# An attention layer on one core: output products held one block behind their transposes, group splits spread, weight subtraction in halves

## The chip, the core and the metric

The kernel runs on one core of a Trainium2 chip. Five engines work in parallel, each through its own queue in order: TensorE (PE, matmuls and transposes; its weight loads are shown as PEld), VectorE (DVE), ScalarE (ACT), GpSimd (POOL) and SyncE (SP, which issues the loads and stores here). SBUF is the working memory; TensorE writes to PSUM, in banks of 128 x 512 float32. The metric is the time of one execution on the device in microseconds; lower is better.

## The reference

One layer of native sparse attention on x of 512 x 1024, float32. With u = RMSNorm(x), a projection gives 16 query heads of 64, three key/value pairs (compressed, selected, window) for 4 groups, gates, and a SiLU path z. With 512 tokens and blocks of 64, all eight blocks are selected, so "selected" is plain causal attention, as is the window of 512.

```
q, kv, g, z = split(u @ w_in)
kc, vc      = compress_kv(k_c, ...), compress_kv(v_c, ...)      # 31 blocks
for branch in (cmp, slc, win):
    p = masked_softmax(q k^T / 8 + bias(distance))
    o[branch] = p v
y   = sum over branches of sigmoid(g) * o * silu(z)
out = x + RMSNorm_post(y @ w_out)
```

## The kernel before

Float32 products are made of two halves: every operand is split into a rounded high part h and the rest l = raw - h, and a product is h*h + l*h + h*l, three matmuls (L144 to L146 for the projections, L809 to L811 for the output). A weight tile of 128 x 1024 is loaded by SP (L103), cast to h (L113 on ScalarE, L115 on VectorE) and subtracted to l (L116). After 126 us the casts are ScalarE's and the subtractions GpSimd's; before, every second tile is VectorE's alone. L425 is one of the three matmuls with which the hidden layer of compress_kv uses such a tile (l times the block).

The attention goes through 28 units: 4 groups of (win 3, win 2, win 1, both 0, slc 1, slc 2, slc 3), where the number is the block of 128 queries; the last group takes its slc units as 3, 2, 1. `qk(u)` makes the scores of four heads (L589), the masked minimum (L601, VectorE) and the exponential (L602, ScalarE), then the factor f (L646) and the widened f times gate (L648, VectorE, two inputs in SBUF). `pv(u)` takes the unit before. For each block j of 128 keys it transposes four heads' probabilities into a PSUM bank (L681), casts them to `pth` (L684, ScalarE), subtracts to `ptl` (L685, VectorE), and multiplies with v (L689 with pth, L690 with ptl) into an accumulator `acc`, which has one bank (`ob`). Product j - 1 is issued behind the transposes of block j; the product of the last block follows in the same unit, behind the two transposes of f (L695). Then ScalarE copies halves of the accumulator out (L700, L701), VectorE adds (L702, L703), and GpSimd multiplies with zs and adds into y (L706, or L708 and L709). `cmp_pv` does the same for the compressed branch behind unit "both" (L752 transposes, L755 cast, L760 to L762 products); `cmp_prep` readies its softmax (L745 is a product of 128 x 16 on VectorE, L746 the one on GpSimd). `split_y` casts and subtracts a quarter of a group's y for the output projection (L777 ScalarE, L778 VectorE); groups 0 to 2 do four quarters in a row behind their last unit.

`weave` alternates the steps of qk(i) and pv(i - 1). Each step yields a cost, and between steps the main loop pulls as many filler steps (projections of later groups, then the output projection `wout`) as a clock of such costs asks for. A tile framework then orders each engine's queue, near the order of the program. A zs tile (three buffers) is free again when `zdone` has its branch.

Of the kernel before, what the change touches and what calls it, by code (L numbers as in the profile page):

```python
# [19 lines left out]
S = 512  # L20
# [4 lines left out]
R = 4  # L25
# [26 lines left out]
def nsa_layer(ctx: ExitStack, tc: tile.TileContext, x, pre_gain, post_gain, table, w_in, w_out,  # L52
# [53 lines left out]
    def split_raw(raw, kn, eh, el, home=None):  # L106
# [9 lines left out]
        el.tensor_tensor(l[:, 0:kn], raw[:, 0:kn], h[:, 0:kn].bitcast(F32), op=ALU.subtract)  # L116
# [547 lines left out]

    def pv(u):
        g, kind, qt = u
        if u == units[g * 7]:
            yt[g] = at.tile([128, 2, S], F32, name="y", tag="y", bufs=1)
        y = yt[g]
        qsl = slice(qt * 128, (qt + 1) * 128)  # L670
        for st in state.pop(u):
            br = st["br"]
            zf = zs[g, br][:, :, qsl]
            acc = ob()
            prev = None
            for j in range(qt + 2):
                if j <= qt:
                    c = st["o"] + j * 128
                    tp = tb()
                    for hh in range(R):  # L680
                        T.transpose(tp[:, hh * 128:(hh + 1) * 128], st["p"][hh][:, c:c + 128], ident)  # L681
                    ph = at.tile([128, S], F32R, name="pth", tag="pth", bufs=2)
                    pl = at.tile([128, S], F32R, name="ptl", tag="ptl", bufs=2)
                    A.copy(ph, tp)  # L684
                    V.tensor_tensor(pl, tp, ph.bitcast(F32), op=ALU.subtract)  # L685
                    yield 690, 440
                if prev is not None:
                    v = vt[:, prev[0], br - 1, g, :]
                    T.matmul(acc, v, prev[1], start=j == 1, stop=False)  # L689
                    T.matmul(acc, v, prev[2], start=False, stop=j == qt + 1)  # L690
                    yield 0, 450
# [5 lines left out]
                prev = (j if br == B_WIN else qt - j, ph, pl)  # L697
            tmp = at.tile([128, 2, 128], F32, name="otmp", tag="otmp", bufs=3)
            av = acc.rearrange("p (a e q) -> p a e q", a=2, e=2)
            A.copy(tmp[0:64], av[64:128, :, 0])  # L700
            A.copy(tmp[64:128], av[0:64, :, 1])  # L701
            V.tensor_tensor(tmp[0:64], av[0:64, :, 0], tmp[0:64], op=ALU.add)  # L702
            V.tensor_tensor(tmp[64:128], av[64:128, :, 1], tmp[64:128], op=ALU.add)  # L703
            eng = V if u == units[-1] else P
            if br == B_WIN:
                eng.tensor_tensor(y[:, :, qsl], tmp, zf, op=ALU.mult)  # L706
            else:
                eng.tensor_tensor(tmp, tmp, zf, op=ALU.mult)  # L708
                eng.tensor_tensor(y[:, :, qsl], y[:, :, qsl], tmp, op=ALU.add)  # L709
            yield 1250, 220  # L710
        if kind == "both":
            zdone.add((g, B_WIN))
            yield from cmp_pv(g)
            zdone.add((g, B_CMP))
            if g == 3:
                split_y(g, 0)
# [31 lines left out]
    def cmp_pv(g):  # L748
        lc, y, vb = lcs[g], yt[g], vbs[g]
# [173 lines left out]
    for i in range(len(units) + 1):  # L923
# [53 lines left out]
```

## Time and profile before

| | us |
|---|---|
| median of 3 runs (lowest to highest) | 479.68 (478.58 to 480.18) |
| profiled execution, its own time | 476.7 |
| span from first to last instruction of that execution | 474.9 |
| TensorE busy | 453.8 |
| VectorE, ScalarE, GpSimd busy | 328.6, 272.3, 178.3 |

In the span, the time before about 11 us is start-up, to about 126 us are the projections and the compression, to about 453 us the units with their filler, and the rest is the end of the output projection. Granted TensorE clock: 0.995 over the span. A row of a timeline has the start, the duration, the engine, the line and the operation with the tiles written and read; idle time ahead of it and what ended it stand in brackets. A matmul is drawn longer than the distance to the next one, since they are pipelined.

### The profile page before, as it was taken

How to read it: one execution, taken by the hardware profiler on the slowest of the kernel's cores; microseconds unless marked ns; L12 is line 12 of the kernel's file. 1: busy time of each engine (PE TensorE's matmuls, PEld its weight loads, DVE VectorE, ACT ScalarE, POOL GpSimd, SP SyncE). 2: the span in 40 equal slices, each digit the busy share in tenths (PEclk: the TensorE clock that was granted, in tenths of full speed). 3: DMA queues.
4: the chain of work that ended last, by engine and by line, in shares of the span. 5: the costliest groups of instructions: out<-in, count | busy, mean ns of one | idle time of the engine just before them, and what ended most of it. 6: DMA issues, size and time to landing. Idle time of an engine off the chain costs nothing.

```text
span 474.9 us, 6859 instructions
## 1 busy us (share of the span) xinstructions
PE 453.8 (96%) x2330; PEld 373.6 (79%) x2330; DVE 328.6 (69%) x788; ACT 272.3 (57%) x643; POOL 178.3 (38%) x139
## 2 busy tenths in 40 slices
PE   5999999999999999999999999999999999997993
PEld 4888788878888878888877887887888887876782
DVE  6789752844667887866857866766886668576576
ACT  5613232535757678766657865755866565546531
POOL 3325543234042635151453324335333244156142
PEclk9999999999999999999999999999999999999997
DMA  8498455351120322220330502032151120124013
GB/s 296 137 88 269 144 168 170 97 176 46 44 90 19 94 88 75 104 60 30 109 92 0 174 5 90 5 108 88 46 177 46 44 85 21 72 80 144 1 44 133
DMA packets 45501, 44.63 MB, mean 94 GB/s; under 512 B 7751, under 2 KB 38471, under 8 KB 45466
## 3 DMA queue, kind: packets, MB, share of 16 engines
q1 hardware_dynamic: 44424, 44.00, 31.2%
q8 instruction: 18, 0.29, 0.2%
q10 hardware_dynamic: 1042, 0.20, 0.2%
q14 instruction: 17, 0.14, 0.1%
HBM read 41.99 MB, written 2.20 MB: 93 GB/s over the span
## 4 chain that ended last, share of the span: by engine, by line
PE 80%; DVE 9%; ACT 5%; issue 3%; POOL 1%; DVEq 0%; POOLq 0%; ACTq 0%
PE ps_pj L144 10%; PE ps_pj L146 10%; PE ps_pj L145 10%; PE ps_s L589 8%; PE ps_t L681 6%; PE ps_o L690 4%; PE ps_o L689 4%; PE ps_s L245 2%; PE ps_s L246 2%; PE ps_s L247 2%; PE ps_pj L809 2%; PE ps_pj L810 2%; PE ps_pj L811 2%; PE ps_pj L245 1%; PE ps_pj L246 1%
## 5 line engine op out<-in xcount | busy, mean ns | idle before, releaser
L116 POOL TENSOR_TENSOR wl<-wr,wh 128x1024 fp32r<-128x1024 f32 x47 | 113.6, 2417 | 147.8 <-ACT wh L113 135.1
L144 PE MATMUL ps_pj<-uh,wh 128*128 128x512 f32 x240 | 98.5, 410 | 0.0
L146 PE MATMUL ps_pj<-ul,wh 128*128 128x512 f32 x240 | 94.3, 393 | 0.0
L145 PE MATMUL ps_pj<-uh,wl 128*128 128x512 f32 x240 | 94.1, 392 | 0.0
L602 ACT ACTIVATE p<-p,nm 128x512 f32<-128x512 f32 (+3 forms) x128 | 71.7, 561 | 26.6 <-DVE nm L601 25.9
L113 ACT CAST wh<-wr 128x1024 fp32r<-128x1024 f32 x47 | 49.2, 1047 | 44.0 <-DMA wr<-in_nsa_w_in_dram 19.0
L685 DVE TENSOR_TENSOR ptl<-ps_t,pth 128x512 fp32r<-128x512 f32 x80 | 55.1, 689 | 26.0 <-ACT pth L684 25.2
L589 PE MATMUL ps_s<-kd,q 128*128 128x512 f32 (+5 forms) x256 | 62.5, 332 | 0.0
L146 PEld LDWEIGHTS ps_pj<-ul,wh 128*128 128x128 f32 x240 | 45.1, 188 | 10.2
L684 ACT CAST pth<-ps_t 128x512 fp32r<-128x512 f32 x80 | 46.0, 575 | 11.5 <-PE ps_t L681 11.1
L589 PEld LDWEIGHTS ps_s<-kd,q 128*128 128x128 f32 x256 | 44.6, 189 | 7.9
L145 PEld LDWEIGHTS ps_pj<-uh,wl 128*128 128x128 f32 x240 | 45.3, 189 | 5.6
L144 PEld LDWEIGHTS ps_pj<-uh,wh 128*128 128x128 f32 x240 | 45.2, 188 | 5.1
L681 PE MATMUL ps_t<-ident,p 128*128 128x128 f32 x320 | 48.2, 272 | 0.0
L681 PEld LDWEIGHTS ps_t<-ident,p 128*128 128x128 f32 x320 | 39.6, 140 | 9.3
L601 DVE CUSTOM_DVE_ANT_0 p<-ps_s,bias 128x128 f32<-128x128 f32 (+3 forms) x80 | 34.6, 446 | 12.0 <-PE ps_s L589 11.3
L689 PE MATMUL ps_o<-pth,vt 128*128 128x512 f32 x80 | 35.5, 444 | 1.5 <-ACT pth L684 1.2
L601 DVE CUSTOM_DVE_ANT_1 p<-ps_s,bias 128x256 f32<-128x256 f32 (+2 forms) x48 | 26.1, 552 | 14.7 <-PE ps_s L589 14.2
L690 PE MATMUL ps_o<-ptl,vt 128*128 128x512 f32 x80 | 32.8, 410 | 3.3 <-DVE ptl L685 3.3
L706 POOL TENSOR_TENSOR y<-otmp,zs 128x256 f32<-128x256 f32 x16 | 11.8, 738 | 57.2 <-DVE otmp L703 57.2
L708 POOL TENSOR_TENSOR otmp<-otmp,zs 128x256 f32<-128x256 f32 x15 | 11.0, 736 | 45.9 <-DVE otmp L703 45.9
L702 DVE TENSOR_TENSOR otmp<-ps_o,otmp 64x256 f32<-64x256 f32 x32 | 13.3, 416 | 18.6 <-ACT otmp L701 17.6
(268 smaller groups left out, 892.8 us busy)
## 6 DMA issues: line engine op xcount, KB each, us to landing
wr<-in_nsa_w_in_dram SPq DMA_DIRECT2D x36, 512.0 KB
wr<-in_nsa_w_in_dram SPq DMA_DIRECT2D x16, 256.0 KB
bias<-toepd SPq DMA_DIRECT2D x16, 256.0 KB
wr<-in_nsa_w_out_dram SPq DMA_DIRECT2D x8, 512.0 KB
xt<-in_x_dram SPq DMA_DIRECT2D x4, 512.0 KB
wr<-in_nsa_cmp_k_w_dram SPq DMA_DIRECT2D x4, 512.0 KB
wr<-in_nsa_cmp_v_w_dram SPq DMA_DIRECT2D x4, 512.0 KB
xr<-in_x_dram SPq DMA_DIRECT2D x8, 256.0 KB
```

The costliest lines, as they stand in the source:

```text
L113: A.copy(h[:, 0:kn], raw[:, 0:kn])
L116: el.tensor_tensor(l[:, 0:kn], raw[:, 0:kn], h[:, 0:kn].bitcast(F32), op=ALU.subtract)
L144: T.matmul(p, a, rh, start=k == 0, stop=False)
L145: T.matmul(p, b, rh, start=False, stop=False)
L146: T.matmul(p, a, rl, start=False, stop=k == KT - 1)
L589: T.matmul(po, qs[h][:, qt * 128:(qt + 1) * 128], kds[h // R][:, i, c0:c0 + n], start=i == 0, stop=i == 1)
L601: V.tensor_tensor_reduce(pd, src, bi, 1.0, BIG, ALU.add, ALU.min, st["nm"][:, hh:hh + 1])
L602: A.activation(po, po, AF.Exp, bias=st["nm"][:, hh:hh + 1], scale=-1.0, accum_out=st["rs"][:, hh:hh + 1])
L681: T.transpose(tp[:, hh * 128:(hh + 1) * 128], st["p"][hh][:, c:c + 128], ident)
L685: V.tensor_tensor(pl, tp, ph.bitcast(F32), op=ALU.subtract)
L689: T.matmul(acc, v, prev[1], start=j == 1, stop=False)
L690: T.matmul(acc, v, prev[2], start=False, stop=j == qt + 1)
```

## The change

Four things change. (1) pv no longer issues a product itself: it puts it in `hold`, and the next block's `flush(0)` issues it behind that block's transposes, also when the next block is another branch's or the next unit's; what follows the last product (copies, additions, zdone, splits) goes with it. The compressed product is held in the same way. (2) The four splits of a group are put in `owed` with counts 1 to 4 and are traced one per block in the units that follow, each queued behind that block's cast on ScalarE. The splits of the last group stay with the product. (3) The weight subtraction is two instructions on two of the four 256-column pieces each, on GpSimd as on VectorE. (4) The costs yielded are the same in sum and lie elsewhere. Banks and buffers are as they were.

```
-        el.tensor_tensor(l[:, 0:kn], raw[:, 0:kn], h[:, 0:kn].bitcast(F32), op=ALU.subtract)
+        for k in range(0, kn, 2):
+            ks = slice(k, k + 2)
+            el.tensor_tensor(l[:, ks], raw[:, ks], h[:, ks].bitcast(F32), op=ALU.subtract)
...
+    hold, owed = [], []
+    def flush(n):
+        while len(hold) > n:
+            yield from hold.pop(0)()
     def pv(u):
...
-            for j in range(qt + 2):
-                if j <= qt:
+            for j in range(qt + 1):
...
-                    A.copy(ph, tp)
+                cast = A.copy(ph, tp)
+                V.tensor_tensor(pl, tp, ph.bitcast(F32), op=ALU.subtract)
+                yield 690, 440
+                for o in list(owed):
+                    o[0] -= 1
+                    if o[0] <= 0:
+                        owed.remove(o)
+                        with tc.issue_after(cast.ins):
+                            o[1]()
+                        yield 420, 0
+                yield from flush(0)
-                if prev is not None:
-                    v = vt[:, prev[0], br - 1, g, :]
-                    T.matmul(acc, v, prev[1], start=j == 1, stop=False)
-                    T.matmul(acc, v, prev[2], start=False, stop=j == qt + 1)
-                    yield 0, 450
...
+                hold.append(lambda st=st, j=j, ph=ph, pl=pl, zf=zf: product(u, st, j, ph, pl, zf))
         if kind == "both":
+            yield from cmp_t(u)
+    def product(u, st, j, ph, pl, zf):
...
+        T.matmul(acc, v, ph, start=j == 0, stop=False)
+        T.matmul(acc, v, pl, start=False, stop=j == qt)
+        yield 0, 450
+        if j < qt:
+            return
...
         if kind == "slc":
             if g == 3:
                 split_y(g, qt)
-            elif u == units[g * 7 + 6]:
-                for t in range(NT):
-                    split_y(g, t)
-                    yield 420, 0
             if u == units[g * 7 + 6]:
+                if g < 3:
+                    owed.extend([t + 1, lambda t=t: split_y(g, t)] for t in range(NT))
                 zdone.add((g, B_SLC))
...
+        if i == len(units):
+            gens[1] = seq(gens[1], flush(0))
```

In the new kernel the products are L714 and L715 (for L689 and L690), the transposes of f L698 (L695), the scores L591 (L589), the subtraction L118 (L116), the split's cast L802 (L777), the projections L146 to L148 (L144 to L146), the output projection L834 to L836 (L809 to L811). The transposes keep L681 and the cast L684.

TensorE at the end of unit win 3 of group 1, before: the first row has the last block's transposes, `pth` in the row before L589 is that block's cast.

```order
L681 MATMUL ps_t<-ident,p 128x128 x4
L689 MATMUL ps_o<-pth,vt 128x512
L690 MATMUL ps_o<-ptl,vt 128x512
L695 MATMUL ps_s<-ident,f_2101 128x128 x2
L689 MATMUL ps_o<-pth,vt 128x512
L589 MATMUL ps_s<-kd,q 128x288 x2
L144 MATMUL ps_pj<-uh_83,wh 128x512
L145 MATMUL ps_pj<-uh_83,wl 128x512
L690 MATMUL ps_o<-ptl,vt 128x512
L146 MATMUL ps_pj<-ul_87,wh 128x512
L681 MATMUL ps_t<-ident,p 128x128 x4
```

The same place now, from the last block's transposes to those of the next unit's first block.

```order
L681 MATMUL ps_t<-ident,p 128x128 x4
L146 MATMUL ps_pj<-uh_82,wh 128x512
L147 MATMUL ps_pj<-uh_82,wl 128x512
L148 MATMUL ps_pj<-ul_86,wh 128x512
L714 MATMUL ps_o<-pth,vt 128x512
L715 MATMUL ps_o<-ptl,vt 128x512
L698 MATMUL ps_s<-ident,f_2121 128x128 x2
L591 MATMUL ps_s<-kd,q 128x288 x2
L681 MATMUL ps_t<-ident,p 128x128 x4
```

Before, the last block's first product stands four rows behind its transposes. Now the two products shown are still the block's before it; the last block's own come 15 rows below the last row shown, behind the next unit's first transposes.

TensorE at the end of unit slc 3 of group 3, where the unit that is woven with it has fewer steps; before:

```order
L689 MATMUL ps_o<-pth,vt 128x512
L690 MATMUL ps_o<-ptl,vt 128x512
L681 MATMUL ps_t<-ident,p 128x128 x4
L689 MATMUL ps_o<-pth,vt 128x512
L690 MATMUL ps_o<-ptl,vt 128x512
L695 MATMUL ps_s<-ident,f_4489 128x128 x2
L809 MATMUL ps_pj<-wh,yhl 128x512
L689 MATMUL ps_o<-pth,vt 128x512
L810 MATMUL ps_pj<-wh,yhl 128x512
```

and now:

```order
L714 MATMUL ps_o<-pth,vt 128x512
L715 MATMUL ps_o<-ptl,vt 128x512
L681 MATMUL ps_t<-ident,p 128x128 x4
L714 MATMUL ps_o<-pth,vt 128x512
L715 MATMUL ps_o<-ptl,vt 128x512
L681 MATMUL ps_t<-ident,p 128x128 x4
L714 MATMUL ps_o<-pth,vt 128x512
L698 MATMUL ps_s<-ident,f_4522 128x128 x2
L591 MATMUL ps_s<-kd,q 128x256
L715 MATMUL ps_o<-ptl,vt 128x512
```

Blocks follow each other here without filler in both; a product now has one product pair and one group of transposes between it and its own transposes.

ScalarE behind the last unit of group 1, before: `yhl` is a split's output, `otmp` the copies out of the accumulator, `wh` a weight cast. The first three splits stand further up; this is the fourth.

```order
L684 CAST pth<-ps_t 128x512
L113 CAST wh<-wr 128x1024
L700 COPY otmp<-ps_o 64x256
L701 COPY otmp<-ps_o 64x256
L567 ACTIVATE zs<-ps_pj 128x512
L777 CAST yhl<-y 128x2x128
L113 CAST wh<-wr 128x1024
L602 ACTIVATE p,rs<-p,nm 128x384
L684 CAST pth<-ps_t 128x512
```

and now, from the copies out of the same unit's accumulator:

```order
L722 COPY otmp<-ps_o 64x256
L723 COPY otmp<-ps_o 64x256
L684 CAST pth<-ps_t 128x512
L604 ACTIVATE p,rs<-p,nm 128x384
L802 CAST yhl<-y 128x2x128
L684 CAST pth<-ps_t 128x512
L802 CAST yhl<-y 128x2x128
L684 CAST pth<-ps_t 128x512
L802 CAST yhl<-y 128x2x128
L604 ACTIVATE p,rs<-p,nm 128x256
L684 CAST pth<-ps_t 128x512
L802 CAST yhl<-y 128x2x128
```

All four splits now stand behind the copies, one to a block and each behind that block's cast; the fourth, which reads the quarter of y that the unit's product completes, stands seven rows further on than the first.

More of the change, by code (lines that the diff above doesn't have):

```diff
@@ L663, in qk @@
             load_bias(g + 1)
+    hold, owed = [], []
+    def flush(n):
+        while len(hold) > n:
+            yield from hold.pop(0)()
     def pv(u):
         g, kind, qt = u
[L667 to L670, printed above, removed]
         for st in state.pop(u):
[L672 to L675, printed above, removed]
-            for j in range(qt + 2):
-                if j <= qt:
[L678 to L686, printed above, removed]
-                if prev is not None:
-                    v = vt[:, prev[0], br - 1, g, :]
-                    T.matmul(acc, v, prev[1], start=j == 1, stop=False)
-                    T.matmul(acc, v, prev[2], start=False, stop=j == qt + 1)
-                    yield 0, 450
+            zf = zs[g, st["br"]][:, :, qt * 128:(qt + 1) * 128]
+            for j in range(qt + 1):
+                c = st["o"] + j * 128
+                tp = tb()
+                for hh in range(R):
+                    T.transpose(tp[:, hh * 128:(hh + 1) * 128], st["p"][hh][:, c:c + 128], ident)
+                ph = at.tile([128, S], F32R, name="pth", tag="pth", bufs=2)
+                pl = at.tile([128, S], F32R, name="ptl", tag="ptl", bufs=2)
+                cast = A.copy(ph, tp)
[9 more added lines that the diff above has]
+                yield from flush(0)
                 if j == qt:
@@ L696, in pv @@
                     V.tensor_tensor(zf, zf, fb[:, 0:256].rearrange("p (a q) -> p a q", a=2), op=ALU.mult)
[L697 to L710, printed above, removed]
-        if kind == "both":
+                    yield 420, 220
+                hold.append(lambda st=st, j=j, ph=ph, pl=pl, zf=zf: product(u, st, j, ph, pl, zf))
@@ new lines, in pv @@
+        if kind == "both":
+            yield from cmp_t(u)
+    def product(u, st, j, ph, pl, zf):
+        g, kind, qt = u
+        br = st["br"]
+        if j == 0:
+            st["acc"] = ob()
+        if j == qt and u == units[g * 7]:
+            yt[g] = at.tile([128, 2, S], F32, name="y", tag="y", bufs=1)
+        acc, y = st["acc"], yt.get(g)
+        v = vt[:, j if br == B_WIN else qt - j, br - 1, g, :]
+        T.matmul(acc, v, ph, start=j == 0, stop=False)
[3 more added lines that the diff above has]
+            return
+        qsl = slice(qt * 128, (qt + 1) * 128)
+        tmp = at.tile([128, 2, 128], F32, name="otmp", tag="otmp", bufs=3)
+        av = acc.rearrange("p (a e q) -> p a e q", a=2, e=2)
+        A.copy(tmp[0:64], av[64:128, :, 0])
+        A.copy(tmp[64:128], av[0:64, :, 1])
+        V.tensor_tensor(tmp[0:64], av[0:64, :, 0], tmp[0:64], op=ALU.add)
+        V.tensor_tensor(tmp[64:128], av[64:128, :, 1], tmp[64:128], op=ALU.add)
+        eng = V if u == units[-1] else P
+        if br == B_WIN:
+            eng.tensor_tensor(y[:, :, qsl], tmp, zf, op=ALU.mult)
+        else:
+            eng.tensor_tensor(tmp, tmp, zf, op=ALU.mult)
+            eng.tensor_tensor(y[:, :, qsl], y[:, :, qsl], tmp, op=ALU.add)
+        yield 840, 0
+        if kind == "both" and br == B_SLC:
@@ L712, in pv @@
             zdone.add((g, B_WIN))
[L713 to L716, printed above, removed]
         if kind == "slc":
@@ L746, in cmp_prep, with cmp_t @@
         P.tensor_tensor(l3, l3, view(rs, 0, [[1, NT * R], [0, CP]]), op=ALU.mult)
[L748 to L749 removed]
+    def cmp_t(u):
+        g = u[0]
+        lc = lcs[g]
         tp = tb()
@@ L757, in cmp_pv, with cmp_product @@
         yield 680, 440
+        yield from flush(0)
+        hold.append(lambda: cmp_product(g, ph, pl))
+    def cmp_product(g, ph, pl):
+        y, vb = yt[g], vbs[g]
         for pr in range(2):
@@ L766, in cmp_pv @@
             yield 1800, 690
+        zdone.add((g, B_CMP))
+        if g == 3:
+            split_y(g, 0)
     def split_y(g, qt):
```

## The prediction, as made before the run

> **What bounds the kernel now.** I read the page's busy shares first, then the table of five stretches (columns: length, then busy time and count of each engine), then TensorE's waits between 126 and 453 us, where the attention runs.
>
> ```profile
> PE 453.8 (96%) x2330; PEld 373.6 (79%) x2330; DVE 328.6 (69%) x788; ACT 272.3 (57%) x643; POOL 178.3 (38%) x139
> 0.00:11.00 11.00, 5.71 (x18) 4.11 (x19) 6.29 (x17) 6.22 (x11) 4.70 (x13) 1.00 0.85 309
> 11.00:126.00 115.00, 113.01 (x621) 96.03 (x620) 75.22 (x124) 47.70 (x97) 41.04 (x24) 1.00 0.54 139
> 126.00:400.00 274.00, 271.81 (x1395) 223.19 (x1394) 197.99 (x561) 183.78 (x458) 101.11 (x77) 1.00 0.23 71
> 400.00:453.00 53.00, 48.80 (x240) 38.60 (x239) 33.80 (x69) 28.68 (x64) 22.62 (x15) 1.00 0.20 70
> 453.00:474.90 21.90, 14.49 (x64) 11.64 (x62) 15.30 (x21) 5.95 (x17) 8.81 (x11) 0.88 0.25 96
> ```
>
> TensorE sets the time: its matmuls are as many before and after (2330), so only its stops can go. Of 21.1 us idle, 5.3 lie before 11 us and 7.4 after 453 us, and the change touches neither end. Left are 2.0 us of 115, 2.2 of 274 and 4.2 of 53. The waits name them (total, times, longest):
>
> ```profile
> PE ps_o L690 <- DVE ptl L685: 3.3, 7, 1.8
> PE ps_o L689 <- ACT pth L684: 1.2, 2, 0.6
> PE ps_pj L809 <- DVE zs L568: 0.8, 1, 0.8
> PE ps_pj L809 <- ACT og L824: 0.5, 1, 0.5
> PE ps_o L760 <- ACT cph L755: 0.2, 1, 0.2
> ```
>
> Twelve stops, 6.0 us. A stop costs more than its idle figure, as this one shows:
>
> ```profile
> 399.08 2.41 POOL L116 TENSOR_TENSOR wl<-wr,wh 128x1024 fp32r<-128x1024 f32 x1
> 399.35 2.17 DVE L745 TENSOR_TENSOR crs<-crs,gate 128x16 f32<-128x16 f32 x1
> ...
> 401.10 0.39 PE L809 MATMUL ps_pj<-wh,yhl 128*128 128x512 f32 x1
> 401.56 0.69 DVE L568 SCALAR_TENSOR_TENSOR zs<-zs,ps_pj 128x512 f32<-128x512 f32 x1
> ...
> 402.30 0.50 PE L809 MATMUL ps_pj<-wh,yhl 128*128 128x512 f32 x1 [0.81 <-DVE zs L568]
> 402.64 0.40 PE L810 MATMUL ps_pj<-wh,yhl 128*128 128x512 f32 x1
> 402.87 0.39 PE L811 MATMUL ps_pj<-wl,yhl 128*128 128x512 f32 x1
> ```
>
> Matmuls without a stop start 0.23 apart (402.64 to 402.87), though each is drawn 0.39 long. From 401.10 to 402.64 two slots (0.46) took 1.54: 1.08 lost where 0.81 is shown. I add 0.27 to every stop: 6.0 + 12 x 0.27 = 9.2 us. The Trainium skill (Perfetto Trace Analysis, Identifying the Most-Contended Engine) calls matmul busy share a poor measure because pipelined matmuls overlap in the trace; by the idle column alone this would be 6.0, and the starts above agree with the rule.
>
> The same fence shows who caused the stop. A VectorE operation on 16 columns took 2.17 us: it began while GpSimd's weight subtraction ran (399.08 to 401.49) and ended just behind it. Two stops before 126 us and the longest of all are of the same kind:
>
> ```profile
> 50.28 2.82 POOL L116 TENSOR_TENSOR wl<-wr,wh 128x1024 fp32r<-128x1024 f32 x1
> ...
> 50.78 3.41 DVE L116 TENSOR_TENSOR wl<-wr,wh 128x1024 fp32r<-128x1024 f32 x1
> ...
> 54.25 0.38 PE L425 MATMUL ps_t<-wl,bh 128*124 128x256 f32 x1 [0.93 <-DVE wl L116]
> ...
> 87.18 3.17 DVE L116 TENSOR_TENSOR wl<-wr,wh 128x1024 fp32r<-128x1024 f32 x1
> ...
> 90.41 0.38 PE L425 MATMUL ps_o<-wl,bh 128*124 128x256 f32 x1 [0.57 <-DVE wl L116]
> ...
> 430.85 4.89 POOL L116 TENSOR_TENSOR w<-wr,w 128x1024 fp32r<-128x1024 f32 x2 [0.72 <-ACT w L113]
> ...
> 431.63 1.88 DVE L648 TENSOR_TENSOR f<-f,gate 128x256 f32<-128x256 f32 x1
> ...
> 434.16 0.50 PE L690 MATMUL ps_o<-ptl,vt 128*128 128x512 f32 x1 [1.76 <-DVE ptl L685]
> ```
>
> The two L425 stops are 0.93 + 0.57 + 2 x 0.27 = 2.0 us; VectorE's subtraction ahead of them took 3.41 and 3.17 us, against 1.23 undisturbed (row below). So 11.3 us can be named, 3.1 of it at the L425 and zs stops and 2.0 in the 1.76 stop, all behind one GpSimd operation.
>
> **The change part by part.**
>
> *Products one block behind, also over unit borders.* Between a block's transposes and its second product lie a ScalarE cast and a VectorE subtraction:
>
> ```profile
> L684 ACT CAST pth<-ps_t 128x512 fp32r<-128x512 f32 x80 | 46.0, 575 | 11.5 <-PE ps_t L681 11.1
> L685 DVE TENSOR_TENSOR ptl<-ps_t,pth 128x512 fp32r<-128x512 f32 x80 | 55.1, 689 | 26.0 <-ACT pth L684 25.2
> 424.61 0.60 PE L681 MATMUL ps_t<-ident,p 128*128 128x128 f32 x4
> ...
> 424.96 0.48 PE L809 MATMUL ps_pj<-wh,yhl 128*128 128x512 f32 x1
> ```
>
> At least 0.58 + 0.69 = 1.3 us, more with anything queued ahead. I walked TensorE's order and gave every 512-column matmul 0.23 us and four transposes 0.35 (424.61 to 424.96). Of 84 blocks (80, and 4 compressed ones), the second product follows its transposes within 3 us in 44 before and 19 now, within 2.3 us in 25 and 10. The product stops are 4.5 + 9 x 0.27 = 6.9 us: 2.0 the locked one, 1.3 the group split below, 3.6 the other six. I let 19/44 of the 3.6 remain: **-2.1**. One block's distance stays short where the other unit has nothing left to interleave (second order piece above): there the 2.0 stop stands, and only the halves help it. The compressed product is likewise later than its cast; its stop is 0.2 + 0.27: **-0.3**. The og stop keeps its code: 0.
>
> *Group splits spread.* Now ScalarE's split stands at the head of its queue until GpSimd has finished y:
>
> ```profile
> 287.68 0.41 ACT L777 CAST yhl<-y 128x256 fp32r<-128x256 f32 x1 [1.51 <-POOL y L709]
> ...
> 290.17 0.49 PE L689 MATMUL ps_o<-pth,vt 128*128 128x512 f32 x1 [0.55 <-ACT pth L684]
> ...
> 290.89 0.50 PE L690 MATMUL ps_o<-ptl,vt 128*128 128x512 f32 x1 [0.23 <-DVE ptl L685]
> ```
>
> The wait holds the casts behind it, and two stops follow (0.55 + 0.23 + 2 x 0.27 = 1.3). In the new order each split stands behind a block's cast, a block after y was asked for: **-1.1**. If y is not done by then, the casts queued behind the split wait as now and the 1.3 stays.
>
> *Subtractions in halves.* The one GpSimd row with a half's shape and two SBUF inputs, and VectorE's undisturbed whole:
>
> ```profile
> L875 POOL TENSOR_TENSOR og<-og,pgain 128x512 f32<-128x512 f32 x3 | 3.9, 1292 | 7.9 <-ACT junk L869 7.9
> ...
> 99.47 1.23 DVE L116 TENSOR_TENSOR wl<-wr,wh 128x1024 fp32r<-128x1024 f32 x1
> ```
>
> A locked VectorE operation then waits at most 1.29 instead of 2.41, 1.12 less. The zs stop (1.08) nearly goes: **-0.9**. At L425 a half also serves the first two of four steps, so these two start another 1.23 - 0.69 = 0.54 earlier; the stops (1.20 and 0.84) mostly go: **-1.4**. Of the 1.76 stop (2.0) I take half: **-1.0**. The price is GpSimd time: 2 x 1.29 against 2.41, +0.17 x 49 = 8 us, beside an engine that is 62% idle and never named as the one TensorE waits for, so 0. Were that cover gone, the 8 us would be paid through late weights. VectorE's eleven subtractions grow by 2 x 0.69 (the shape of the L685 row) less 1.23, 0.15 each, within 115 us of which it is busy 75: 0, at most 1.7. The cost of the halves is thus between 0 and 10; I take 0, since no stop of TensorE names GpSimd.
>
> *What is asked for later.* The zs tiles and the last weight loads on SP's queue are released with the products, a block later. The last weights were split by 435.74 (the 430.85 row) and are first used here:
>
> ```profile
> 452.29 0.39 PE L809 MATMUL ps_pj<-w,y 128*128 128x512 f32 x1
> ```
>
> That is 16.5 us of cover for a block of a few us: 0. Late zs tiles can hold back filler matmuls; rival (5) has that.
>
> *Bank as it was.* One accumulator bank; the next accumulation waits until ScalarE and VectorE have emptied it. From the last product's start to the end of L703:
>
> ```profile
> 150.84 0.40 PE L690 MATMUL ps_o<-ptl,vt 128*128 128x512 f32 x1
> ...
> 154.30 0.43 DVE L703 TENSOR_TENSOR otmp<-ps_o,otmp 64x256 f32<-64x256 f32 x1
> ...
> 436.12 0.39 PE L690 MATMUL ps_o<-ptl,vt 128*128 128x512 f32 x1
> ...
> 437.75 0.43 DVE L703 TENSOR_TENSOR otmp<-ps_o,otmp 64x256 f32<-64x256 f32 x1
> ```
>
> 2.06 us with free queues, 3.89 in the worst place. By the slots above, the shortest gaps to the next accumulation are 1.97, 2.06, 2.20, 2.20 and 2.48 before, and 1.69 (into the last unit), 1.92, 2.15, 2.15, 2.43, then 2.84, 2.89, 2.92 and 3.35 now; gaps under 4.3 us rise from 10 to 21. At 2.06 two stops cost 0.37 + 0.14 + 2 x 0.27 = 1.0 now, and one cost 0.09 + 0.27 before: 0.7. I take **+0.8**, near the row with free queues; the upper end is rival (4).
>
> **Sum.** -2.1 - 0.3 - 1.1 - 0.9 - 1.4 - 1.0 + 0.8 = -6.0 us. The profiled execution took 476.7 us (span 474.9 and 1.8 around it): 470.7 on its own scale. The median of the runs is 3.0 above it, so I take 479.7 - 6.0 = **473.7 us**. About 0.3% (1.4 us) is what a measurement of this kernel tells from no change.
>
> **Rivals.** (1) *All stops go.* -11.3: 468.4. For it: lags under 0.16 us show no idle and would go too. Against: the stretches without filler keep short distances.
> (2) *The queues, not the distances, set the waits.* Then product stops come back elsewhere and only the lock terms less the bank remain: -0.9 - 1.4 - 1.0 + 0.8 = -2.5: 477.2. For it: the 290.17 stop had a cast late behind other work. Against: six stops have no such lock.
> (3) *GpSimd's second half takes the port before the waiting VectorE operation.* Then that waits 2 x 1.29 = 2.58, as long as now, and -0.9 and -1.0 are lost, with part of the -1.4: -3.7: 476.0. Against: in the 430.85 pair VectorE, waiting since 431.63, ended at 433.51, between the two operations. The Trainium skill (SBUF — State Buffer, Who interferes with whom) says the pair shared by VectorE and GpSimd is held for a whole instruction and that issue order decides who blocks; it leaves open who is next, and the trace agrees with the holding: 2.17 us for 16 columns.
> (4) *The bank becomes the bound: slower.* In the new order the evacuation stands nearer to the next accumulation. If it takes 3.5 us at borders, the nine shortest gaps lose 9.2 (each 3.5 less its gap) + 9 x 0.27 = 11.6 against the -6.8 of the other terms: +4.8, 484.5. It decides from about 3.0 us on. For it: the 150.84 row. Against: 436.12, at a border of the same kind.
> (5) *Nothing moves on balance*, since later releases of zs hold back filler: 479.7.
>
> **Chances.** Forecast 0.50, (1) 0.12, (2) 0.20, (3) 0.08, (4) 0.05, (5) 0.05. Faster: 0.50 + 0.12 + 0.8 of (2) and (3) (0.22) = 0.84, less 0.03 for what no row shows: 0.81. Same: 0.12, slower: 0.07. The range goes from 469.5, near the full sum, to 479.0, over (2) and (3); about 0.2 lies outside.
>
> **What would show it.** Right: TensorE's stops at the two product lines fall from nine to about four; no VectorE operation on 16 to 256 columns over 1.5 us; no L425 stop; ScalarE no longer idle for y at the group borders before the last. Wrong: stops at the first product of a unit that wait for the otmp additions, at both/win and at the last unit first (4); VectorE still 2 us beside two halves in a row (3); as many product stops at larger distances (2).

## The result and the profile after

| | before | after |
|---|---|---|
| median of the timed runs (lowest to highest), us | 479.93 (478.58 to 480.90), 4 runs | 472.03 (470.77 to 472.55), 4 runs |
| ratio after to before, 95% interval | | 0.9833 (0.9802 to 0.9865) |
| profiled execution, its own time; its span, us | 476.7; 474.9 | 471.89; 470.1 |
| GpSimd busy, us | 178.3 | 188.6 |

Measured again later beside other kernels, the changed kernel took 472.06 us (471.26 to 473.91, 4 runs) against 479.44: 0.9843 (0.9821 to 0.9865). The forecast was 473.7. The four runs of before are the three of the first table and one more, 480.90.

The page of the changed kernel gives TensorE the same 2330 matmuls and nearly the same busy time as before:

```profile
PE 453.6 (96%) x2330; PEld 376.6 (80%) x2330; DVE 331.0 (70%) x799; ACT 274.7 (58%) x643; POOL 188.6 (40%) x188
```

So what changed is TensorE's stops. The table of stretches of the changed kernel (length, then PE, PEld, DVE, ACT and POOL busy with counts, granted clock, DMA) shows where:

```profile
11.00:126.00 115.00, 114.03 (x610) 97.29 (x611) 74.03 (x131) 46.28 (x94) 44.79 (x38) 0.99 0.54 141
126.00:400.00 274.00, 272.62 (x1408) 225.44 (x1406) 206.12 (x564) 187.44 (x459) 109.75 (x106) 1.00 0.24 71
400.00:453.00 53.00, 52.04 (x259) 42.56 (x259) 32.51 (x74) 31.25 (x70) 23.61 (x24) 1.00 0.21 70
453.00:470.10 17.10, 9.68 (x43) 7.64 (x41) 12.51 (x17) 3.85 (x12) 6.61 (x9) 0.88 0.32 123
```

From 126 to 400 us TensorE is now idle for 1.4 us instead of 2.2, from 400 to 453 for 1.0 instead of 4.2. The list of its waits between 11 and 460 us (total, times, longest) names what is left:

```profile
PE ps_pj L247 <- ACT uh L327: 1.4, 2, 1.1
PE ps_o L714 <- DVE otmp L725: 0.9, 3, 0.4
PE ps_o L714 <- ACT pth L684: 0.6, 2, 0.4
PE ps_t L427 <- DVE wl L118: 0.4, 1, 0.4
PE ps_o L427 <- DVE wl L118: 0.4, 1, 0.4
PE ps_o L782 <- DVE otmp L725: 0.3, 1, 0.3
PE ps_o L715 <- DVE ptl L685: 0.2, 1, 0.2
```

The 1.76 us stop, the zs stop and the og stop are gone. Product stops for a late cast or subtraction are three instead of nine. Four stops are new: they wait for the otmp additions, that is for the accumulator bank (the row of L782 is the compressed product). Both L427 stops (L425 before) are still there, smaller.

**A ruler that the start-up doesn't bend.** The times of one kernel spread over 1 to 4.5 us, as much as the parts of the change that are to be told apart. Three rows in each trace avoid this: TensorE's first matmul of the hidden layer, its first transposes of probabilities, and its last matmul. Before, and then the changed kernel in its second measurement:

```profile
46.05 0.28 PE L423 MATMUL ps_t<-wh,bh 128*124 128x256 f32 x1
...
122.04 0.49 PE L681 MATMUL ps_t<-ident,p 128*128 128x128 f32 x3
...
467.10 0.39 PE L811 MATMUL ps_pj<-w,y 128*128 128x512 f32 x1
```

```profile
48.16 0.28 PE L425 MATMUL ps_t<-wh,bh 128*124 128x256 f32 x1
...
123.39 0.38 PE L681 MATMUL ps_t<-ident,p 128*128 128x128 f32 x2
...
461.67 0.39 PE L836 MATMUL ps_pj<-w,y 128*128 128x512 f32 x1
```

The first stage (call it the front) takes 122.04 - 46.05 = 75.99 us before and 75.23 now. The second (the units), to the end of the last matmul, takes 467.49 - 122.04 = 345.45 before and 462.06 - 123.39 = 338.67 now. In the changed kernel's first profile they were 75.19 and 338.66, so here the ruler repeats to a few hundredths. The table below has two cases where it doesn't: the units when the clock halves in them, and one front of 77.31 us where six others with the same whole subtraction have 75.99 to 76.04. By the ruler the change is worth 0.8 + 6.8, together 7.5 us. What lies before the front differs by 2 us between two profiles of the same kernel and says nothing on the change; the last section shows a part of the reason.

### The profile page after: what moved, and what is told of

Read it like the earlier page. It is cut to its first block, busy times and chain, and to the rows that moved or that the text cites. A ratio compares the mean times of both kernels' runs of the same rounds, so it can differ in the third digit from the quotient of the medians.

```text
span 470.1 us, 6941 instructions
## 1 busy us (share of the span) xinstructions
PE 453.6 (96%) x2330; PEld 376.6 (80%) x2330; DVE 331.0 (70%) x799; ACT 274.7 (58%) x643; POOL 188.6 (40%) x188
## 4 chain that ended last, share of the span: by engine, by line
PE 80%; DVE 7%; ACT 7%; issue 2%; DMA 2%; POOL 1%; SPq 0%; DVEq 0%; POOLq 0%; ACTq 0%
PE ps_pj L148 10%; PE ps_pj L146 10%; PE ps_pj L147 10%; PE ps_s L591 8%; PE ps_t L681 6%; PE ps_o L715 4%; PE ps_o L714 4%; PE ps_s L247 2%; PE ps_s L248 2%; PE ps_s L249 2%; PE ps_pj L247 2%; PE ps_pj L248 2%; PE ps_pj L249 2%; PE ps_pj L834 2%; PE ps_pj L835 2%
## 5 line engine op out<-in xcount | busy, mean ns | idle before, releaser
L118 POOL TENSOR_TENSOR wl<-wr,wh 128x512 fp32r<-128x512 f32 x94 | 123.0, 1328 | 139.8 <-ACT wh L113 123.7
L146 PE MATMUL ps_pj<-uh,wh 128*128 128x512 f32 x240 | 99.0, 413 | 0.0
L148 PE MATMUL ps_pj<-ul,wh 128*128 128x512 f32 x240 | 94.1, 392 | 0.0
L604 ACT ACTIVATE p<-p,nm 128x512 f32<-128x512 f32 (+3 forms) x128 | 71.5, 560 | 25.1 <-DVE nm L603 24.4
L591 PE MATMUL ps_s<-kd,q 128*128 128x512 f32 (+5 forms) x256 | 62.9, 334 | 0.0
L684 ACT CAST pth<-ps_t 128x512 fp32r<-128x512 f32 x80 | 46.3, 580 | 26.6 <-PE ps_t L681 26.0
L148 PEld LDWEIGHTS ps_pj<-ul,wh 128*128 128x128 f32 x240 | 45.1, 188 | 10.2
L591 PEld LDWEIGHTS ps_s<-kd,q 128*128 128x128 f32 x256 | 43.9, 189 | 7.6
L146 PEld LDWEIGHTS ps_pj<-uh,wh 128*128 128x128 f32 x240 | 45.2, 188 | 5.9
L681 PE MATMUL ps_t<-ident,p 128*128 128x128 f32 x320 | 47.9, 272 | 0.0
L681 PEld LDWEIGHTS ps_t<-ident,p 128*128 128x128 f32 x320 | 39.6, 140 | 9.0
L714 PE MATMUL ps_o<-pth,vt 128*128 128x512 f32 x80 | 33.9, 424 | 1.6 <-DVE otmp L725 0.9
L715 PE MATMUL ps_o<-ptl,vt 128*128 128x512 f32 x80 | 32.3, 404 | 0.5 <-DVE ptl L685 0.2
L569 ACT ACTIVATE zs<-ps_pj 128x512 f32<-128x512 f32 x22 | 13.1, 597 | 19.4 <-PE ps_pj L148 19.3
```

Source lines behind the costliest of these rows:

```text
L118: el.tensor_tensor(l[:, ks], raw[:, ks], h[:, ks].bitcast(F32), op=ALU.subtract)
L146: T.matmul(p, a, rh, start=k == 0, stop=False)
L148: T.matmul(p, a, rl, start=False, stop=k == KT - 1)
L591: T.matmul(po, qs[h][:, qt * 128:(qt + 1) * 128], kds[h // R][:, i, c0:c0 + n], start=i == 0, stop=i == 1)
L604: A.activation(po, po, AF.Exp, bias=st["nm"][:, hh:hh + 1], scale=-1.0, accum_out=st["rs"][:, hh:hh + 1])
L714: T.matmul(acc, v, ph, start=j == 0, stop=False)
```

## The experiments

"Held" is part (1) of the change together with the moved costs of part (4), which no run separates, "spread" part (2), "halves" part (3). Ratios are to the kernel before on the same chip; front and units are the two stages above, from one profile each. A star marks profiles in which the granted clock halved once for some 3.4 us within the units; in the kernel before that cost 346.83 - 345.45 = 1.4 us.

| kernel | median us (runs) | ratio, 95% interval | front | units |
|---|---|---|---|---|
| before | see above | 1 | 75.99 | 345.45 |
| before again (e0) | 479.87 (1) | | 76.01 | 346.83* |
| halves (e1) | 475.54 (6) | 0.9921 (0.9895 to 0.9947) | 75.21 | 341.94 |
| spread (f1) | 476.84 (7) | 0.9931 (0.9900 to 0.9962) | 76.00 | 344.78* |
| held (f2) | 476.13 (6) | 0.9913 (0.9895 to 0.9932) | 76.00 | 343.70* |
| held + halves (e3) | 475.72 (6) | 0.9938 (0.9917 to 0.9959) | 75.21 | 342.33 |
| held + spread (e2) | 471.34 (5) | 0.9832 (0.9806 to 0.9858) | 77.31 | 338.17 |
| held + spread again (g3) | 471.08 (5) | 0.9845 (0.9813 to 0.9876) | 76.04 | 338.21 |
| all three = after, again (f4) | 472.06 (4) | 0.9843 (0.9821 to 0.9865) | 75.23 | 338.67 |
| after, VectorE's halves only (g1) | 473.06 (6) | 0.9881 (0.9853 to 0.9909) | 76.45 | 338.21 |
| after, GpSimd's halves only (g2) | 469.80 (6) | 0.9828 (0.9800 to 0.9857) | 75.55 | 338.70 |
| after, two accumulator banks (f3) | 470.13 (4) | 0.9795 (0.9779 to 0.9811) | 74.82 | 337.27 |
| the same, whole subtraction (g4) | 471.08 (5) | 0.9851 (0.9824 to 0.9879) | 75.99 | 337.50 |

**Halves alone** (the kernel before with this edit):

```
-        el.tensor_tensor(l[:, 0:kn], raw[:, 0:kn], h[:, 0:kn].bitcast(F32), op=ALU.subtract)
+        for k in range(0, kn, 2):
+            ks = slice(k, k + 2)
+            el.tensor_tensor(l[:, ks], raw[:, ks], h[:, ks].bitcast(F32), op=ALU.subtract)
```

> The kernel before with the weight subtraction in halves and nothing else. Theory A (the terms of the forecast add up): the locked stops shrink, -0.9 - 1.4 - 1.0 = -3.3 us, about 476.6 against 479.9; the two L425 stops (0.93 and 0.57 idle) fall under 0.4 each and the product stops without a lock stay. Theory B (the halves are what works, the held products are idle): most of the 7.9 us, 473 or less. Theory C (only the distance of the products counts): within 1 us of 479.9.

Measured: 3.5 us less in the units, 0.8 in the front. The zs stop goes, the og stop too, which the forecast had at 0, and the 1.76 us stop shrinks to 0.67. Timeline of this kernel at that place:

```profile
431.01 2.70 POOL L118 TENSOR_TENSOR w<-wr,w 128x512 fp32r<-128x512 f32 x2 [0.57 <-ACT w L113]
...
431.78 0.79 DVE L650 TENSOR_TENSOR f<-f,gate 128x256 f32<-128x256 f32 x1
...
433.23 0.50 PE L692 MATMUL ps_o<-ptl,vt 128*128 128x512 f32 x1 [0.67 <-DVE ptl L687]
```

The VectorE operation that took 1.88 us beside two whole subtractions ends here after 0.79, between GpSimd's halves. In the kernel before, halves alone do what was claimed for them at the zs stop and the 1.76 us stop. The two L425 stops fall to 0.4 each, and the front gains 0.8 us, not the 1.4 of the forecast.

**Held and spread, subtraction whole** (the changed kernel with the first line above put back):

> The changed kernel with the weight subtraction whole again. Theory A: it loses the 3.3 us of the locked stops and keeps the rest, about 475.3 against 472.0; VectorE operations on 16 to 256 columns of about 2 us come back and stops of 0.5 to 1.8 us behind them. Theory B: back near 479. Theory C: 472, no change.

Measured: 471.34, as fast as with the halves, and the zs stop and the 1.76 us stop are gone here too, although every GpSimd subtraction is whole. These are the rows of its waits that lie in the units:

```profile
PE ps_o L712 <- DVE otmp L723: 0.8, 3, 0.4
PE ps_o L712 <- ACT pth L682: 0.6, 2, 0.4
PE ps_o L780 <- DVE otmp L723: 0.3, 1, 0.3
```

In the units it is even 0.5 us shorter than the changed kernel (338.17 against 338.67). What the halves alone are worth, 3.5 us in the units, and what holding is worth there are thus largely the same stops, and can't be added. Only the front shows the whole subtraction, in this profile with a longer stop than before (0.93 in its repetition, g3):

```profile
53.04 3.40 DVE L116 TENSOR_TENSOR wl<-wr,wh 128x1024 fp32r<-128x1024 f32 x1
...
56.50 0.38 PE L425 MATMUL ps_t<-wl,bh 128*124 128x256 f32 x1 [1.61 <-DVE wl L116]
```

**Held and halves, four splits in a row:**

```
-                    owed.extend([t + 1, lambda t=t: split_y(g, t)] for t in range(NT))
+                    for t in range(NT):
+                        split_y(g, t)
+                        yield 420, 0
```

> The changed kernel with the four splits of a group in a row behind its last product, as before. Theory A: +1.1 us, about 473.1, with ScalarE idle for y at the head of its queue at the group borders and a product stop behind it. Rival: the held products have distance enough to hide the late casts, so within 0.5 us of 472.0.

Measured: 3.7 us more in the units than the changed kernel. Here is one group border in its timeline:

```profile
269.78 0.60 PE L681 MATMUL ps_t<-ident,p 128*128 128x128 f32 x4
270.09 0.41 ACT L804 CAST yhl<-y 128x256 fp32r<-128x256 f32 x1 [1.26 <-POOL y L731]
270.40 0.58 ACT L684 CAST pth<-ps_t 128x512 fp32r<-128x512 f32 x1
...
271.03 0.50 PE L714 MATMUL ps_o<-pth,vt 128*128 128x512 f32 x1 [0.65 <-ACT pth L684]
```

ScalarE waits 1.26 us for GpSimd's y at the last split, and the cast of the next unit's block, queued behind it, comes too late for TensorE. Holding makes this worse: the split follows the group's last product, which now lies behind the next unit's first transposes, so it stands where that unit's casts are wanted. The group lines of ScalarE's split between 126 and 453 us (busy, mean ns, idle before) say the same. Before, held + halves, spread alone, and the changed kernel, in this order:

```profile
L777 ACT CAST yhl<-y 128x256 fp32r<-128x256 f32 x12 | 4.7, 402 | 10.2 <-POOL y L709 10.0 <-PE ps_s L589 0.2
```

```profile
L804 ACT CAST yhl<-y 128x256 fp32r<-128x256 f32 x12 | 4.8, 402 | 12.7 <-POOL y L731 12.7
```

```profile
L784 ACT CAST yhl<-y 128x256 fp32r<-128x256 f32 x12 | 4.9, 405 | 0.0
```

```profile
L802 ACT CAST yhl<-y 128x256 fp32r<-128x256 f32 x12 | 4.8, 404 | 0.0
```

**The kernel before once more**, for the spread between two of its profiles:

> The kernel before once more, for a second profiled execution, since the first one's own time (476.7) lies below all its timed runs (478.6 to 480.9). If the extra 3 us are stops that come and go with the meeting of GpSimd and VectorE, this trace shows more or longer locked operations than the first and a span near 477 to 478; if it is another state of the chip, all matmuls are a little longer and the stops are the same.

It took 479.87 us where the first profile took 476.7. The front is the same (76.01) and so are the marked stops in the units. Of the difference, 1.8 us lies before the front and 1.4 in the units. In each of the two the clock halved once for 3.4 us (last section), about 1.4 us each, so matmuls at half clock make up most of it.

**Spread alone** (the kernel before with the `owed` list; products and subtraction as before):

```
-                    A.copy(ph, tp)
+                    cast = A.copy(ph, tp)
...
+                    for o in list(owed):
...
-                for t in range(NT):
-                    split_y(g, t)
-                    yield 420, 0
+                owed.extend([t + 1, lambda t=t: split_y(g, t)] for t in range(NT))
```

> The kernel before with the four splits of groups 0 to 2 spread over the next unit's blocks; products and subtraction as they were. Theory P (spreading and holding are a pair; alone, spreading takes away only the split stops it can be seen to cause before, 0.55 + 0.23 idle at 290 us): ScalarE's idle time before L777 on yhl falls from 10.2 us to under 1, the six other product stops, the zs stop and both L425 stops stay, 1.0 to 1.5 us less than before, about 477.6 where before is 479.0. Theory Q (ScalarE standing at the borders costs 3 to 4 us by itself, since casts behind it come late without a visible stop): 475 to 476.

Measured: 476.84 us, between the two theories; the ratio of 0.9931 is some 3.3 us of 479.4 (1.8 to 4.8). The units, less 1.4 for the half clock, are 343.4, 2.0 us less than before. The 1.4 is the cost in another profile and taken over here, and in the next run. So spreading is worth 2 us without holding.

**Held alone:**

> The changed kernel with the four splits in a row and the subtraction whole: holding alone. Theory P: as with the halves but in a row (475.7), the border stops of 3.9 us remain, the zs stop and the 1.76 stop go, the two L425 stops of 2.0 us come back: 476.5 to 477.5, about 2 less than before. Rival R (halves do nothing for the time, the front's stops are made up elsewhere): 475.5, as with the halves. Rival S (the forecast's additive terms: held -2.4, bank +0.8): 477.4, with a zs stop and a stop over 1 us in the 433 us neighbourhood still there.

Measured: 476.13 us, 0.9913, just under the range of Theory P. The units, less 1.4, are 342.3, 3.1 us less than before. With halves as well they are 342.33, so on held products the halves add nothing in the units. Nor does holding add anything to the halves there: halves alone have 341.94. From 342.3 to 338.2 (e2), spreading is worth 4.1 us on top of holding, twice what it is worth alone. Theory P named the right mechanism (the border stops stay, the zs and the 1.76 us stops go).

Of the eight combinations one is missing: halves and spread without holding. Were their gains in the units, 3.5 and 2.0 us, to add up, it would have 339.9 us there, 1.3 more than the changed kernel. What holding is worth beside the other two isn't measured.

**Two accumulator banks**, the second taken from the scores:

```
-    sb = lambda: bank("s", 3)
+    sb = lambda: bank("s", 2)
...
-    ob = lambda: bank("o", 1)
+    ob = lambda: bank("o", 2)
```

> The changed kernel with two accumulator banks and two instead of three for the scores. Theory P: the four first-product stops that wait for the otmp additions (1.2 us idle + 4 x 0.27 = 2.2 us) go and scores find a bank in time: 469.8 where the changed kernel is 472.0. Rival T (the third score bank is needed): stops at L591 or L698 waiting for the minimum or the exponential come in for at least as much: 472.0 or more.

Measured: 470.13, and 1.4 us less in the units, not 2.2. All four bank stops are gone. A new one shows the price, in the timeline of this kernel:

```profile
262.77 0.42 DVE L699 TENSOR_TENSOR zs<-zs,ps_s 128x256 f32<-128x256 f32 x1
...
263.25 0.73 PE L591 MATMUL ps_s<-kd,q 128*128 128x512 f32 x2 [0.61 <-DVE zs L699]
```

The scores wait until VectorE has emptied the bank with the transposes of f. Both theories held in part: the bank stops go, and the third score bank is missed, for less. On the whole subtraction (g4 against g3 in the table) the second bank is worth 0.7 us in the units. By its ratio this is the fastest kernel of the study, but its interval overlaps that of GpSimd's halves alone.

**The changed kernel again:**

> The changed kernel itself, beside the others on one chip: 472.0 (470.8 to 472.6 at the first measurement); from the first transposes of the units to the last instruction of TensorE 338.7 us, as in its first profile, within 0.5. If holding and spreading with the whole subtraction (471.34 before) is really level with it, the halves are worth nothing on top; if this comes out at 470 or less, they are worth about the 1.4 us of the two L425 stops.

Stages and time repeat (above). The time alone doesn't settle what the halves are worth, so four runs took them apart.

**Halves on one engine each, and none:**

```
+        n = 2 if el is V else kn
-        for k in range(0, kn, 2):
-            ks = slice(k, k + 2)
+        for k in range(0, kn, n):
+            ks = slice(k, k + n)
```

> The changed kernel with VectorE's weight subtractions in halves and GpSimd's whole. Theory U (at L425 most of the gain is GpSimd's shorter hold on VectorE; VectorE's own halves only give the first two steps their data 0.54 us earlier): the two L425 stops shown are 0.4 to 0.6 idle each more than the changed kernel's 0.38 and 0.36; from the first L425 stage to TensorE's end 414.3 to 414.8 us, where the changed kernel has 413.9 and the whole subtraction 415.25; 472.0 to 472.6. Rival W (VectorE's halves do it all): both stops as in the changed kernel, 413.4, and 471.5, GpSimd's 8 us of extra work being saved.

> The changed kernel with GpSimd's weight subtractions in halves and VectorE's whole. Theory U: VectorE waits for half a subtraction instead of a whole one, so both L425 stops are smaller than with both whole (1.61 and 0.58 idle), at 0.9 or less each; 414.2 to 414.8 us from the first L425 stage to the end, 472.0 to 472.6. Rival W: stops as with both whole, 415.2 us.

> The changed kernel with the whole subtraction, once more, to see whether the 471.34 that stood against 472.03 and 472.06 holds although its L425 stops are 1.4 us longer. Theory X (the halves are worth those 1.4 us; the median was a matter of start-up, which shifts by 1.8 us from run to run): 472.5 to 473.5 here. Theory Y (what the halves win at L425 they give back, so that they are worth nothing once the products are held): 471.0 to 472.2, and TensorE reaches its first L425 step earlier than in the kernels with halves, near 47.2 us instead of 48.2 to 49.4.

> The changed kernel with two accumulator banks, two for the scores, and the whole subtraction: the same question with the banks that did better (470.13 with halves). Theory X: 471.0 to 472.0, L425 stops of 1.5 to 2.2 us idle together. Theory Y: 469.3 to 470.4.

With one accumulator bank the units agree: 338.17 to 338.21 wherever GpSimd subtracts whole, 338.66 to 338.70 wherever it subtracts in halves. Most of these 0.5 us lie at three products, at 348, 428 and 431 us, which start 0.10 to 0.15 us later and wait for VectorE's subtraction. That GpSimd's longer busy time is the cause is argued, not shown; with two banks the units are 0.2 us shorter with halves (337.27 against 337.50). From the front's start to TensorE's end, VectorE's halves alone take 76.45 + 338.21 = 414.66 us and GpSimd's alone 75.55 + 338.70 = 414.25, as Theory U has it and not Rival W. The two L425 stops are 0.5 and 1.2 us with the one, 0.95 and under 0.15 with the other. The fronts by themselves are weaker evidence: there is one profile of each, and the whole subtraction has given 76.04 and 77.31.

In the medians, GpSimd's halves alone are 3.3 us faster than VectorE's alone; by the stages they should be 0.4 faster. Their profiled executions are 4.0 apart, and 3.5 of it lie before the front (49.48 against 45.95 us to the first matmul of the front). One window of each shows most of this (the third figure from the end is the granted clock); VectorE's halves first, GpSimd's second:

```profile
23.50:30.50 7.00, 7.00 (x35) 6.98 (x35) 3.06 (x10) 1.37 (x4) 0.52 (x1) 0.51 1.01 119
```

```profile
23.50:30.50 7.00, 7.00 (x54) 6.65 (x54) 5.16 (x15) 1.94 (x3) 0.53 (x2) 1.00 1.05 119
```

Half clock (0.51) over the whole window in the one, full clock in the other: 35 matmuls against 54 in the same 7 us. All six profiles of kernels with halves on VectorE have at least one such stretch before the front, and three of the eight without. Whether VectorE's halves bring it about isn't settled: no row shows what sets it off there. Nor does it account for every time: one timed run of VectorE's halves had a granted clock of 0.997 over its span, as the profiled run of GpSimd's halves had, and took 473.04 us against 469.39.

The comparison of whole and halved subtraction gives no single answer either. With one bank the whole one (g3) is 1.0 us below the changed kernel in the median and level by the ratio to before (0.9845 against 0.9843), where Theory X had it above. With two banks the whole one (g4) is slower, as Theory X has it: 0.9851 against 0.9795, intervals apart. By the ruler, front and units together, the halves are worth 0.4 us with one bank (413.90 against 414.25) and 1.4 with two (412.09 against 413.49), all or most of it in the front, from one profile each. What the halves are worth in the time of the changed kernel is within about 1 us of nothing. Two banks with GpSimd's halves alone weren't tried.

## Why the prediction was right, and where it was not

To compare its terms with the trace I took, for each pair of neighbouring TensorE rows, what their starts lie apart beyond the slot (0.229 us for 512 columns, 0.09 for a transpose). The levels hang on the slots taken for narrower matmuls, by 1 us or more; the differences hang on them by some 0.2 us. From the first transposes to 460 us this loss was 24.4 us before and is 17.8 now; in pieces over 0.15 us it was 11.6 and is 6.4. Sorted by what TensorE waited for:

| term | forecast | before | now | seen |
|---|---|---|---|---|
| products late for cast or subtraction (with the 1.76 us stop and the border) | -2.1 - 1.0 - 1.1 = -4.2 | 9.3 | 4.6 | -4.7 |
| compressed product late | -0.3 | 0.6 | 0 | -0.6 |
| zs stop | -0.9 | 1.0 | 0 | -1.0 |
| og stop | 0 | 0.7 | 0 | -0.7 |
| accumulator bank | +0.8 | 0 | 1.9 | +1.9 |
| pieces under 0.15 us, no stop marked | 0 | 12.8 | 11.4 | -1.4 |
| L425 stops, by the front | -1.4 | | | -0.8 |
| sum | -6.0 | | | -7.3 |

**What held.** Only TensorE's stops could go, and with 2330 matmuls as before that is where the time came from. The sum of 6.0 compares with 7.5 us between the landmarks, and 7.4 to 7.9 between the medians. The base was right too: the profiled execution of before stood 3.2 us under its own repetition, and had neither of the two stretches of half clock that this one had.

**The near sum is in part luck.** Taken in the order held, spread, halves, the ruler gives -3.1, -4.1 and -0.3 us. The forecast had -2.1 - 0.3 + 0.8 = -1.6 for holding with its bank, -1.1 for spreading and -3.3 for the halves. The first two were too small by 1.5 and 3.0, the last too large by 3.0, and the last two cancel. The table above, sorted by the row that waits, can't show this: it has the halves' -1.0 and the spread's -1.1 in one row with the held products.

**Where the parts were put down wrongly.** The terms of -0.9 for the zs stop and -1.0 for half of the 1.76 us stop, because a half locks VectorE for a shorter time, named a true effect: e1 shows it, 1.88 to 0.79 us. But they were added to the term of the held products. The prediction said of the last group's place that "there the 2.0 stop stands, and only the halves help it". This is the step that failed: held alone and held + spread have the subtraction whole, and no stop for a late subtraction is over 0.31 us in their units. The rows show what took its place. Before, VectorE takes the locked operation (431.63) ahead of the subtraction that the product waits for (433.43), whose cast stands behind an exponential on ScalarE (431.28 behind 430.67). In the changed kernel the cast (427.74) stands ahead of the exponential (428.21), and so the subtraction ahead of the locked operation, in its timeline:

```profile
427.91 5.19 POOL L118 TENSOR_TENSOR w<-wr,w 128x512 fp32r<-128x512 f32 x4 [0.78 <-ACT w L113]
...
428.35 0.69 DVE L685 TENSOR_TENSOR ptl<-ps_t,pth 128x512 fp32r<-128x512 f32 x1 [1.90 <-ACT pth L684]
...
429.16 1.54 DVE L650 TENSOR_TENSOR f<-f,gate 128x256 f32<-128x256 f32 x1
```

Held alone has the same order, whole subtractions and all (432.95 ahead of 433.76); spread alone has the old one, and its stop of 1.76 us. So holding took this stop by turning the order on two other queues. The prediction did not read these; at this place it weighed TensorE's distance and the lock. At the zs stop it was a meeting that moved: in held + spread the product of 16 columns starts 1.5 us after a whole subtraction of GpSimd's (398.04 and 396.55) instead of 0.3, and takes 0.95 us instead of 2.17. Neither holding nor spreading aimed at that.

The mark "no VectorE operation on 16 to 256 columns over 1.5 us" was missed, here by 0.04 us and by 0.01 in one more row (152.60 us), and it was a poor mark. Of the other marks, "no L425 stop" was missed too: both stay, at 0.38 and 0.36 us. The stops at the two product lines fell from nine to six, not to about four, since three of the six wait for the bank. For a pair of parts that serve one wait, the smaller one's term should have been conditional on the other.

**The spread term (-1.1) was mis-sized.** It was read from the stops of the old order. It is 2.0 us alone and 3.7 to 4.1 with held products, since holding without spreading puts the splits onto the next unit's casts: ScalarE's idle time there is 10.2 us before, 12.7 with holding and halves, 0.0 with spreading. The mark "ScalarE no longer idle for y at the group borders before the last" came as said.

**The bank term (+0.8) was mis-sized: 1.9.** The prediction took 2.06 us from the last product to the end of the additions. One of the four stops in the changed kernel's timeline:

```profile
248.30 0.39 PE L715 MATMUL ps_o<-ptl,vt 128*128 128x512 f32 x1
...
248.97 0.69 DVE L685 TENSOR_TENSOR ptl<-ps_t,pth 128x512 fp32r<-128x512 f32 x1
...
250.37 0.43 DVE L725 TENSOR_TENSOR otmp<-ps_o,otmp 64x256 f32<-64x256 f32 x1
...
250.94 0.47 PE L714 MATMUL ps_o<-pth,vt 128*128 128x512 f32 x1 [0.44 <-DVE otmp L725]
```

From 248.30 to 250.80 are 2.50 us: the next block's subtraction and a product with zs stand ahead of the additions on VectorE. The waits for the otmp additions were the sign named for rival (4), and they came, in four places. But 2.50 lies under the 3.0 us from which that rival would have decided, and a second bank, net of a score bank, wins back 1.4 us in the units (f3), or 0.7 with the whole subtraction (g4).

**The L425 term (-1.4) was mis-sized: 0.8.** It let VectorE wait for one half of GpSimd's. The changed kernel's timeline shows it waiting for two:

```profile
53.16 1.72 POOL L118 TENSOR_TENSOR wl<-wr,wh 128x512 fp32r<-128x512 f32 x1
...
53.65 1.77 DVE L118 TENSOR_TENSOR wl<-wr,wh 128x512 fp32r<-128x512 f32 x1
...
54.83 1.74 POOL L118 TENSOR_TENSOR wl<-wr,wh 128x512 fp32r<-128x512 f32 x1
...
55.34 1.77 DVE L118 TENSOR_TENSOR wl<-wr,wh 128x512 fp32r<-128x512 f32 x1
...
57.17 0.39 PE L427 MATMUL ps_t<-wl,bh 128*124 128x256 f32 x1 [0.38 <-DVE wl L118]
```

The halves of the two engines take turns. VectorE's pair ends 3.46 us after its start, against 3.41 before; only the first half is early. This is not rival (3), in which GpSimd's second half would have gone ahead of VectorE. The Trainium skill (SBUF — State Buffer, Who interferes with whom) calls the pair shared by the two engines an exclusive lock; it speaks of holding for the whole instruction where VectorE runs in a two-port mode, and says that an instruction with two inputs in SBUF contends with GpSimd's reads. These rows, with two inputs in SBUF, agree with a hold of a whole instruction: each VectorE half ends 0.54 us after the GpSimd half that it met.

**The halves' price was put at 0, within 0 to 10 us.** With one bank it is 0.5 us in the units, if those are GpSimd's doing (338.66 to 338.70 against 338.17 to 338.21): its 94 halves take 1.33 us each where a whole one took 2.42, about 0.24 us more a tile and 10 us in all, nearly all under cover.

**Rivals.** (1), all stops go, fails on the three late products and four bank stops, but its remark that lags without a mark would shrink too was worth 1.4 us. (2) is seen only in the last group, where stops at 429 to 444 us stay.

## What to carry to other kernels

Price the parts of a change on top of each other, not each against the old trace: two parts that serve the same wait pay once (halves, 3.5 us in the units alone, nothing there behind held products), and one that moves the obstacle of another pays twice (spreading, 2 us alone, 4 with holding). Holding a consumer back also moves everything queued behind it, so look at what its tail lands on, and at the order that the other engines' queues take by it. To tell parts of 1 us apart in a kernel whose times spread over 3, compare the stretch between two instructions that all versions share, and take more than one profile of each.

## What the hardware showed beyond that

**Stretches of half clock.** The changed kernel, before the front; windows around one such stretch, and then matmuls ahead of it and in it:

```profile
20.00:25.90 5.90, 5.66 (x41) 4.38 (x40) 4.09 (x12) 2.81 (x7) 3.02 (x3) 0.99 0.16 40
25.90:29.30 3.40, 3.40 (x18) 3.40 (x18) 1.01 (x6) 0.07 (x1) 0.00 (x0) 0.51 0.99 173
```

```profile
25.48 0.28 PE L247 MATMUL ps_pj<-uh,wh 128*128 128x256 f32 x1
25.60 0.28 PE L248 MATMUL ps_pj<-uh,wl 128*128 128x256 f32 x1
...
26.50 0.41 PE L247 MATMUL ps_pj<-uh,wh 128*128 128x256 f32 x1
26.71 0.41 PE L248 MATMUL ps_pj<-uh,wl 128*128 128x256 f32 x1
```

For 3.4 us the granted clock is 0.51, and matmuls start 0.21 us apart instead of 0.12. It is some 16 matmuls times 0.09, 1.4 to 1.5 us. Before the front there were none, one or two (6.8 us on end) in the fourteen profiles, and this is a part of why the times of one kernel spread; the first profile of before, with none at all, was short. With none TensorE reached the front at 45.95 to 48.22 us, with one at 47.09 to 48.83, with two at 49.42 and 49.48. These ranges overlap, so what lies before the front varies by some 2 us for other reasons too, which stay open.

**A long stop may cost twice.** In the units a stretch came in three profiles: the repetition of before, spread alone and held alone. Each began within 1.1 us after a stop of TensorE of 1.15 to 1.76 us, and those are three of the only four profiles with a stop over 1 us in the units; the ten without such a stop show none. In the front, two stops as long had no such stretch behind them (1.61 us at 56.50 in e2, 1.15 us at 95.02 in g1), and before the front stretches came with no stop over 0.9 us between 12 us and them. So this is a coincidence in three places of six, and no rule. The repetition of before, and then the first profile of before at the same place, behind the same stop:

```profile
436.90:440.40 3.50, 3.50 (x12) 2.82 (x11) 1.57 (x5) 1.14 (x3) 0.54 (x1) 0.51 0.57 212
```

```profile
434.40:437.80 3.40, 3.40 (x20) 2.86 (x20) 1.92 (x6) 1.22 (x4) 1.35 (x1) 1.00 0.66 237
```

If the stop is what sets the stretch off, removing it also removed a chance of another 1.4 us, which no list of waits shows. The Trainium skill (TensorE: Matmul & The Clock Gate, Part 1: The HAM clock gate) describes a clock that passes half its pulses after an idle window of about 3.4 us, the window running freely. The length agrees with these rows (3.4 us at 0.51). The idle time doesn't: no stop ahead of them was longer than 1.76 us. That the window's phase decides whether such a stop is punished would fit the two profiles above, but no row shows the phase; it stays open.
